# One scan chain, eight buffers for the projected inputs and TensorE-only adaLN slices in a hybrid S5 / DeltaNet / mixture-of-experts layer

## The chip, the cores and the metric

The kernel runs on one core of a Trainium2 chip. A time is the device time of one execution in microseconds (us); several executions are timed and their median is told. One further execution is recorded by the profiler, and all rows below come from that one.

## What is computed

One layer of a trunk, with 512 latent tokens `x` and 256 context tokens `ctx` of width 2048, all in fp32. Cut to what matters here:

```
mod = silu(c) @ ada_w + ada_b            # 2048 x 12288: shift, scale, gate, twice
sh1, sc1, g1, sh2, sc2, g2 = split(mod)
hin  = concat([ctx * (1 + csc1) + csh1, x * (1 + sc1) + sh1])
proj = hin @ w_in                        # first 1024 columns: S5, the rest: DeltaNet
# S5, 64 groups of 16 channels, 64 complex states, forward and backward
bu = einsum(b_bar, u); h[t] = lam_bar * h[t-1] + bu[t]; y = einsum(c_mat, h).real
s5 = g * sigmoid(g @ glu_w + glu_b),  g = gelu(y_forward + y_backward + d_skip * u)
dn = gated_delta_rule(...)               # 8 heads of 128, chunks of 64, both directions
x  = layer_norm(alpha * x + g1 * (concat([s5, dn]) @ w_out))
x  = layer_norm(alpha * x + g2 * expert_choice_ffn(x * (1 + sc2) + sh2))   # 16 experts
```

The context stream itself is not an output; the S5 scans and the DeltaNet recurrences pass through it first.

## The kernel before

The program runs in stages. `phase_in` (0 to some 205 us) makes the first two adaLN vectors (its loads are issued at L281, its matmuls are L284), normalizes the inputs and projects the S5 columns. A projection (helper lines L387 to L398) loads a weight tile `wr`, casts it on ScalarE to `wh` (L388), takes the rest `wl = wr - wh` on GpSimd (L390), and adds three products on TensorE: L396, L397, L398. Beside 512 latent columns (a matmul of 512 columns) some also have 256 context columns.

`put_u` then stores the projected S5 inputs: for each of eight row blocks, ScalarE (L1724) and VectorE (L1725) copy the accumulators into a tile `ue`, and a DMA (L1727) writes it to DRAM. `ue` has two buffers. `transposed` turns B and C coefficients by way of TensorE, a ScalarE copy into `tpd` (two buffers, L909) and a store.

The S5 stage works in blocks of 8 scan positions, 94 of them in a row for context and latent together. `s5_states` (L1108) makes the input of each state: 32 steps of two groups each, with loads of `P` and `B`, products on VectorE (L1124 to L1128) and GpSimd (L1123, L1126), four matmuls L1133 and ScalarE copies into the tile `VH`. `s5_scan` (L1149) goes along `VH`: 94 steps of three VectorE operations, each of which needs the result of the one before (L1156 the product, L1157 and L1158 the two additions). The groups are split into two chains of 32 by the table `CHAINS`: the scan of the first 32 groups follows the first 16 state steps in the program, and the scan of the other 32 the last 16. `s5_local` (L1161, matmuls L1173) and `s5_outputs` (L1177: ScalarE copies `Hs`, 256 matmuls L1192, an addition on VectorE) make the outputs, which go through DRAM (`yd`) to `s5_gelu` (L1219) and `gates` (L490 to L499). In the DeltaNet stage (L572 is the first matmul of its first head, some 805 us) eight heads pass through a front, an inversion and a scan, and the output projection follows. The mixture of experts runs from some 1620 us to the end.

Two kinds of work are filler and are laid beside all this: the DeltaNet projections (a list `PRE` of those that come before the DeltaNet stage, `REST` inside it), and the adaLN slices for `g1, sh2, sc2, g2`: 16 slices of 512 columns (four of the 2048 columns of each). `ada_chunk` loads a slice in eight loads of two row blocks by 512 columns (`aw`, 512 KB each, L213) and multiplies them on TensorE with the vector `cT` in a 128x32 tile of the array (L217); the 16 row blocks go round four column tiles, two at a time. The slices with numbers 2 and 3 (`AV`) go to `ada_vec` instead: 16 multiply-adds of 128x512 on VectorE (L255) and a small matmul.

The order on each engine is not the program's: a scheduler sets it at build time, from the program's dependencies, its pools of buffers and a model of the durations. Any edit in the stages up to 1590 us therefore moves filler about.

Of the kernel before, what the change touches and what calls it, by code (L numbers as in the profile page):

```python
# [11 lines left out]
F32 = mybir.dt.float32  # L12
# [9 lines left out]
D = 2048  # L22
# [19 lines left out]
def ap(t, off, dims):  # L42
    return bass.AP(tensor=t.tensor, offset=t.offset + off, ap=[list(d) for d in dims])
# [6 lines left out]
def mp(K, shape=(128, 4, 128), tag="mp"):  # L50
    return K.ps.tile(list(shape), F32, name=tag, tag=tag, bufs=K.banks[tag])
# [151 lines left out]
    nc.vector.tensor_scalar(K.nega, K.nega, -1.0, None, op0=MUL)  # L203


def ada_chunk(K, I, pool, c0, nk=8, bufs=2):

    nc = K.nc
    src = I["ada_w"]
    pa = mp(K, (128, 512), K.adb)  # L210
    for k0 in range(0, KT, nk):
        aw = pool.tile([128, nk, 512], F32, name="aw", tag="aw", bufs=bufs)
        nc.sync.dma_start(aw, ap(src, c0 + k0 * 128 * 6 * D, [[6 * D, 128], [128 * 6 * D, nk], [1, 512]]))  # L213
        for kk in range(nk):
            k = k0 + kk
            j = k % 4
            nc.tensor.matmul(pa[32 * j:32 * j + 32], K.cT[:, k], aw[:, kk], start=k < 4, stop=k >= 12, tile_position=(0, 32 * j))  # L217
    return pa


def turn(K, pool, pa, pm):
# [9 lines left out]
def ada_cols(K, I, pool, c0, dst, m, **kw):  # L231

    nc = K.nc
    pa = ada_chunk(K, I, pool, c0, **kw)
    pm = mp(K, (128, 512), K.adb)[:, :4 * m].rearrange("p (a b) -> p a b", a=4)
    turn(K, pool, pa, pm)
    cb = c0 // 128
    nc.vector.tensor_tensor(dst, pm, bc(K.cols[:, cb:cb + 4][:, :, None], [128, 4, m]), op=ADD)
    yield from ()


def ada_vec(K, I, pool, c0, dst, m, nk, bufs):

    nc = K.nc
    V = nc.vector
    acc = pool.tile([128, 512], F32, name="part2", bufs=1)
    for k0 in range(0, KT, nk):
        aw = pool.tile([128, nk, 512], F32, name="aw", tag="aw", bufs=bufs)
        nc.sync.dma_start(aw, ap(I["ada_w"], c0 + k0 * 128 * 6 * D, [[6 * D, 128], [128 * 6 * D, nk], [1, 512]]))
        for kk in range(nk):  # L250
            c = K.cT[:, k0 + kk, 0:1]
            if k0 + kk == 0:
                V.tensor_scalar(acc, aw[:, kk], c, None, op0=MUL)
            else:
                V.scalar_tensor_tensor(acc, aw[:, kk], c, acc, op0=MUL, op1=ADD)  # L255
        if AVY:
            yield
    t = pool.tile([128, 512], F32, name="part", bufs=1)
    V.transpose(t, acc)
    r = pool.tile([128, 16, 1], F32, name="part3", bufs=1)  # L260
    V.tensor_reduce(r[:, :, 0], t.rearrange("p (a c) -> p a c", c=32), axis=AX.X, op=ADD)
    pm = mp(K, (128, 4, 1), K.adb)
    for q in range(4):
        nc.tensor.matmul(pm[32 * q:32 * q + 32], K.sel32, r.rearrange("p (a q) m -> p q a m", q=4)[:, q], start=True, stop=True, tile_position=(0, 32 * q))
    cb = c0 // 128
    V.tensor_tensor(dst, pm, K.cols[:, cb:cb + 4][:, :, None], op=ADD)

# [605 lines left out]
BN = 2  # L875
CP = (0, 1)
SV = (999,999,999)
AV = (2, 3)
AVY = 0
MA = (4, (1,))  # L880
YB = 3
STEP0 = [1, 1, 2]
# [1 line left out]
NP = 6  # L884
QZ = [(0, 0), (0, 1)] + [(w, h + (0 if w else 2)) for h in range(6) for w in (3, 0)] + [(3, 6), (3, 7)]
PRE, REST = QZ[:NP], QZ[NP:]
NKA = (2,3)
AR = 2
NWS = 13
PARTS = (0,4),(4,4),(8,4),(12,3),(15,1)  # L890
NN = [0, 2, 2, 0, 0]
UB = 2
NA = sum(NN)
NKB = (2,3)

CHAINS = ((0, 32, "vector"), (32, 32, "vector"))
OPB = 4
AWB = 3
XTB = 1
# [3 lines left out]
def transposed(K, p, src, n, dst):  # L903

    pt = mp(K, (128, n, 128))
    for i in range(n):
        K.nc.tensor.transpose(pt[:, i], src[:, 128 * i:128 * i + 128], K.ident)
    t = p.tile([128, n, 128], F32, name="tpd", bufs=2)
    K.nc.scalar.copy(t, pt)  # L909
    K.nc.sync.dma_start(dst, t)  # L910

# [392 lines left out]
def ada_rest(K, I):  # L1304

    nc = K.nc
    cols = [K.const.tile([128, KT, 1], F32, name=f"ada{s}") for s in range(2, 6)]
    K.g1, K.sh2, K.sc2, K.g2 = cols
    for s, dst in zip(range(2, 6), cols):
        for ch in range(4):  # L1310
            f = ada_vec if 4 * (s - 2) + ch in AV else ada_cols
            yield from f(K, I, K.ada, s * D + ch * 512, dst[:, 4 * ch:4 * ch + 4], 1, nk=K.nka[0], bufs=K.nka[1])
            yield
    nc.vector.tensor_scalar(K.sc2, K.sc2, 1.0, None, op0=ADD)
    yield
# [362 lines left out]
def hybrid_trunk_kernel(tc, I, O):  # L1678
# [3 lines left out]
    with ExitStack() as es:  # L1682
# [36 lines left out]
        K.hin = [(K.yh("hi"), hinl.tile([128, KT, NL], F32R, name="lo")),  # L1719
                 tuple(hinc.tile([128, KT, NC], F32R, name=w) for w in ("hic", "loc"))]  # L1720

        def put_u(i, pl, pc):
            ue = K.up.tile([128, 8, 96], F32, name="ue", bufs=2)
            nc.scalar.copy(ue[:, :, 32:96].rearrange("p s (r w) -> p w s r", r=8), pl.rearrange("p (w s r) -> p w s r", w=8, s=8))  # L1724
            nc.vector.tensor_copy(ue[:, :, 0:32].rearrange("p s k -> p k s"), pc.rearrange("p (k s) -> p k s", s=8))  # L1725
            o = (32 * (i % 2) + i // 2) * 12288
            nc.sync.dma_start(ap(K.us5, o, [[4 * 12288, 8], [768, 16], [1, 768]]), ue.rearrange("p a b -> p (a b)"))  # L1727

        s5k = vk.enter_context(left("s5k"))
        with left("acc") as accp:  # L1730
            uts, par = phase_in(K, I, accp, s5k)
            for i, (pl, pc) in enumerate(uts):
                put_u(i, pl, pc)
        pss.close()
        K.ps = pss.enter_context(tc.tile_pool(name="psx", bufs=1, space=PSUM, reuse_waits="tile"))
        K.adb = "ada"
# [169 lines left out]
```

## Time and profile before

| | us |
|---|---|
| median of three runs (lowest, highest) | 2703.14 (2702.12, 2708.47) |
| the profiled execution | 2703.15 |
| its span in the trace | 2701.4 |
| TensorE busy | 2467.7 (91%) |
| VectorE busy | 1300.9 (48%) |
| ScalarE busy | 717.7 (27%) |
| GpSimd busy | 783.6 (29%) |

The times of the stages in this execution: copies of `put_u` 213.6 to 244.4 us, states 444 to 575, first operation of a scan at 511.4 and last at 687.2, S5 outputs 652.8 to 714.8, first DeltaNet head 805.3, mixture of experts from 1620. A stage's busy times are read from the windows, what an engine waited for from the waits, and the price of one instruction from the timeline. The granted clock of TensorE over the span is 0.96 of its upper level. Ends of matmuls are modelled, so the time from one start to the next tells more than the duration.

### The profile page before, as it was taken

How to read it: one execution, taken by the hardware profiler on the slowest of the kernel's cores; microseconds unless marked ns; L12 is line 12 of the kernel's file. 1: busy time of each engine (PE TensorE's matmuls, PEld its weight loads, DVE VectorE, ACT ScalarE, POOL GpSimd, SP SyncE). 2: the span in 40 equal slices, each digit the busy share in tenths (PEclk: the TensorE clock that was granted, in tenths of full speed). 3: DMA queues.
4: the chain of work that ended last, by engine and by line, in shares of the span. 5: the costliest groups of instructions: out<-in, count | busy, mean ns of one | idle time of the engine just before them, and what ended most of it. 6: DMA issues, size and time to landing. Idle time of an engine off the chain costs nothing. (4 is left out here: it accounts for less than half of the span.)

```text
span 2701.4 us, 41223 instructions
## 1 busy us (share of the span) xinstructions
PE 2467.7 (91%) x16062; PEld 1541.3 (57%) x16062; DVE 1300.9 (48%) x2831; ACT 717.7 (27%) x1611; POOL 783.6 (29%) x747
## 2 busy tenths in 40 slices
PE   7998989899878989899999859999999999999994
PEld 4665778778756766566667724434444444444441
DVE  3362685899577677767877560411111101010106
ACT  2223233534544344443333330201010101010111
POOL 2341275631255464545454410400000000000002
PEclk9998999999988999899999979999999999999997
DMA  9956847766654456777763287998999999999893
GB/s 281 323 176 166 266 148 210 195 163 163 187 158 123 116 174 197 239 224 227 225 194 85 63 319 276 362 382 339 390 384 389 383 390 366 406 366 408 350 406 128
DMA packets 444317, 698.73 MB, mean 259 GB/s; under 512 B 91288, under 2 KB 271001, under 8 KB 443097
## 3 DMA queue, kind: packets, MB, share of 16 engines
q1 hardware_dynamic: 438745, 693.82, 74.6%
q10 hardware_dynamic: 5376, 2.26, 0.4%
q8 instruction: 127, 2.08, 0.3%
q14 instruction: 69, 0.57, 0.1%
HBM read 646.12 MB, written 49.87 MB: 258 GB/s over the span
## 5 line engine op out<-in xcount | busy, mean ns | idle before, releaser
L390 POOL TENSOR_TENSOR wl<-wr,wh 128x512 fp32r<-128x512 f32 (+2 forms) x248 | 335.2, 1354 | 609.3 <-ACT wh L388 577.9
L1522 PE MATMUL mp<-ws,selT 128*64 128x512 f32 x1992 | 468.9, 594 | 0.5 <-ACT selT L1461 0.5
L1522 PEld LDWEIGHTS mp<-ws,selT 128*64 128x64 f32 x1992 | 176.2, 137 | 265.7 <-issue 258.8
L1556 PE MATMUL mp<-ws,hT 128*64 128x512 f32 x896 | 298.2, 603 | 0.0
L1606 POOL TENSOR_TENSOR yp<-ypf,yp 128x512 fp32r<-128x512 f32 x31 | 39.7, 1280 | 875.0 <-ACT yp L1605 875.0
L388 ACT CAST wh<-wr 128x512 fp32r<-128x512 f32 (+2 forms) x249 | 150.5, 605 | 351.3 <-PE pp L397 140.1
L396 PE MATMUL pp<-hi,wh 128*128 128x512 f32 (+1 forms) x528 | 222.0, 420 | 18.4 <-ACT wh L388 18.4
L398 PE MATMUL pp<-hi,wl 128*128 128x512 f32 (+1 forms) x528 | 221.6, 420 | 16.3 <-POOL wl L390 16.3
L397 PE MATMUL pp<-lo,wh 128*128 128x512 f32 (+1 forms) x528 | 217.4, 412 | 0.0
L1528 DVE SCALAR_TENSOR_TENSOR hid<-hid,mp 128x512 f32<-128x512 f32 x16 | 11.0, 688 | 354.9 <-ACT hid L1527 354.1
L1604 DVE SCALAR_TENSOR_TENSOR ypf<-mp,gc,g2r 128x512 f32<-128x512 f32 x32 | 24.0, 751 | 318.5 <-issue 184.9
L1556 PEld LDWEIGHTS mp<-ws,hT 128*64 128x64 f32 x896 | 83.5, 136 | 141.9 <-issue 130.2
L1618 DVE TENSOR_TENSOR acc<-acc,pp 128x512 f32<-128x512 f32 x124 | 79.1, 683 | 162.7 <-PE pp L1616 162.7
L1458 PEld LDWEIGHTS pp<-oh,mixed 128*128 128x128 f32 x1024 | 123.5, 197 | 57.3 <-issue 57.3
L1461 ACT ACTIVATE selT<-pp,colB,colA 128x128 f32<-128x128 f32 x128 | 48.3, 457 | 341.8 <-PE pp L1458 341.8
L1458 PE MATMUL pp<-oh,mixed 128*128 128x128 f32 x1024 | 136.8, 287 | 1.3 <-DVE oh L1450 1.3
L398 PEld LDWEIGHTS pp<-hi,wl 128*128 128x128 f32 (+1 forms) x528 | 102.7, 195 | 49.1 <-POOL wl L390 25.3
L396 PEld LDWEIGHTS pp<-hi,wh 128*128 128x128 f32 (+1 forms) x528 | 104.0, 197 | 37.3 <-ACT wh L388 23.0
L397 PEld LDWEIGHTS pp<-lo,wh 128*128 128x128 f32 (+1 forms) x528 | 104.1, 197 | 18.3 <-issue 4.7
L1527 ACT ACTIVATE hid<-mp 128x512 f32<-128x512 f32 x16 | 9.6, 597 | 381.6 <-PE mp L1522 381.6
L217 PE MATMUL ada<-aw,cT 128*32 128x512 f32 x448 | 100.1, 633 | 11.8 <-DMA aw<-in_ada_w_dram 7.3
L396 PE MATMUL pp<-oph,wh 128*128 128x512 f32 x240 | 98.9, 417 | 6.7 <-DVE Z L666 3.5
(583 smaller groups left out, 4819.2 us busy)
## 6 DMA issues: line engine op xcount, KB each, us to landing
ws<-in_exp_w_dram SPq DMA_DIRECT2D x375, 1024.0 KB
aw<-in_ada_w_dram SPq DMA_DIRECT2D x184, 512.0 KB
wr<-in_w_in_dram SPq DMA_DIRECT2D x157, 256.0 KB
wr<-in_w_out_dram SPq DMA_DIRECT2D x52, 256.0 KB
cl<-CL SPq DMA_DIRECT2D x8, 1024.0 KB
P<-tp SPq DMA_DIRECT2D x32, 256.0 KB
B<-tb SPq DMA_DIRECT2D x32, 256.0 KB
CLo<-cl SPq DMA_DIRECT2D x16, 512.0 KB
```

What stands on the lines that cost most here:

```text
L217: nc.tensor.matmul(pa[32 * j:32 * j + 32], K.cT[:, k], aw[:, kk], start=k < 4, stop=k >= 12, tile_position=(0, 32 * j))
L388: nc.scalar.copy(wh, wr)
L390: (nc.vector if K.nsp % K.sv == 1 else nc.gpsimd).tensor_tensor(wl, wr, wh.bitcast(F32), op=SUB)
L396: T.matmul(out, wh, hi, start=st, stop=False, **kw)
L397: T.matmul(out, wh, lo, start=False, stop=False, **kw)
L398: T.matmul(out, wl, hi, start=False, stop=sp, **kw)
L1458: T.matmul(pg[:, j], K.y[:, k, b], ohf[:, b], start=(b == 0), stop=(b == 3))
L1461: A.activation(S.selT[:, k], pg[:, j], AF.Identity, scale=K.A[:, k:k + 1], bias=K.B[:, k:k + 1])
L1522: T.matmul(acc4[2 * w + c][64 * a:64 * a + 64], S.selT[:, k, 64 * a:64 * a + 64], ws[w, a][:, kk, 512 * c:512 * c + 512], start=(k == 0), ...
L1556: T.matmul(acc[c][64 * a:64 * a + 64], S.hT[:, f0 + f, 64 * a:64 * a + 64], ws[a][:, f, 512 * c:512 * c + 512], start=(f0 + f == 0), stop= ...
L1606: (nc.vector if end else nc.gpsimd).tensor_tensor(t[:, 1], y, t[:, 0].bitcast(F32), op=SUB)
L1618: K.nc.vector.tensor_tensor(K.acc[:, b, s], K.acc[:, b, s], ps, op=ADD)
```

## The change

Four edits. `ada_chunk` goes through each half of 256 columns with four loads of four row blocks by 256 columns (again eight loads of 512 KB for a slice), and the four matmuls of a load use the four column tiles. `ada_vec` goes: all 16 slices take the TensorE way. `CHAINS` holds one chain of 64 groups, so the whole scan stands behind all 32 state steps, and its operations are twice as wide (256, 128 and 128 columns) and half as many. `ue` has eight buffers in a pool of its own that is closed after the stores, and `tpd` four. `ADY` is 0, so the added `yield None` is never reached.

```diff
-def ada_chunk(K, I, pool, c0, nk=8, bufs=2):
+def ada_chunk(K, I, pool, c0, bufs=3):
 
     nc = K.nc
     src = I["ada_w"]
     pa = mp(K, (128, 512), K.adb)
-    for k0 in range(0, KT, nk):
-        aw = pool.tile([128, nk, 512], F32, name="aw", tag="aw", bufs=bufs)
-        nc.sync.dma_start(aw, ap(src, c0 + k0 * 128 * 6 * D, [[6 * D, 128], [128 * 6 * D, nk], [1, 512]]))
-        for kk in range(nk):
-            k = k0 + kk
-            j = k % 4
-            nc.tensor.matmul(pa[32 * j:32 * j + 32], K.cT[:, k], aw[:, kk], start=k < 4, stop=k >= 12, tile_position=(0, 32 * j))
-    return pa
+    for c in range(0, 512, 256):
+        for k0 in range(0, KT, 4):
+            aw = pool.tile([128, 4, 256], F32, name="aw", tag="aw", bufs=bufs)
+            nc.sync.dma_start(aw, ap(src, c0 + c + k0 * 128 * 6 * D, [[6 * D, 128], [128 * 6 * D, 4], [1, 256]]))
+            for j in range(4):
+                nc.tensor.matmul(pa[32 * j:32 * j + 32, c:c + 256], K.cT[:, k0 + j], aw[:, j], start=k0 == 0, stop=k0 == 12, tile_position=(0, 32 * j),
+                                 skip_group_check=True)
+        if ADY:
+            yield None
+    yield pa
...
-    pa = ada_chunk(K, I, pool, c0, **kw)
+    for pa in ada_chunk(K, I, pool, c0, **kw):
+        if pa is None:
+            yield
...
-def ada_vec(K, I, pool, c0, dst, m, nk, bufs):
-
-    nc = K.nc
-    V = nc.vector
-    acc = pool.tile([128, 512], F32, name="part2", bufs=1)
-    for k0 in range(0, KT, nk):
-        aw = pool.tile([128, nk, 512], F32, name="aw", tag="aw", bufs=bufs)
-        nc.sync.dma_start(aw, ap(I["ada_w"], c0 + k0 * 128 * 6 * D, [[6 * D, 128], [128 * 6 * D, nk], [1, 512]]))
-        for kk in range(nk):
-            c = K.cT[:, k0 + kk, 0:1]
-            if k0 + kk == 0:
-                V.tensor_scalar(acc, aw[:, kk], c, None, op0=MUL)
-            else:
-                V.scalar_tensor_tensor(acc, aw[:, kk], c, acc, op0=MUL, op1=ADD)
...
-    V.transpose(t, acc)
...
-AV = (2, 3)
-AVY = 0
+ADY = 0
...
-NKA = (2,3)
+NKA = 3
...
-NKB = (2,3)
-
-CHAINS = ((0, 32, "vector"), (32, 32, "vector"))
+NKB = 3
+
+CHAINS = ((0, 64, "vector"),)
...
-    t = p.tile([128, n, 128], F32, name="tpd", bufs=2)
+    t = p.tile([128, n, 128], F32, name="tpd", bufs=4)
...
-            f = ada_vec if 4 * (s - 2) + ch in AV else ada_cols
-            yield from f(K, I, K.ada, s * D + ch * 512, dst[:, 4 * ch:4 * ch + 4], 1, nk=K.nka[0], bufs=K.nka[1])
+            yield from ada_cols(K, I, K.ada, s * D + ch * 512, dst[:, 4 * ch:4 * ch + 4], 1, bufs=K.nka)
...
-        def put_u(i, pl, pc):
-            ue = K.up.tile([128, 8, 96], F32, name="ue", bufs=2)
+        def put_u(i, pl, pc, pool):
+            ue = pool.tile([128, 8, 96], F32, name="ue", bufs=8)
...
-            for i, (pl, pc) in enumerate(uts):
-                put_u(i, pl, pc)
+            with left("ues") as pool:
+                for i, (pl, pc) in enumerate(uts):
+                    put_u(i, pl, pc, pool)
```

The scheduler then gives another order from about 205 us to about 1590 us. In the rows below the changed kernel has its own line numbers (L1698 is L1724 of before, L364 is L388, L1131 to L1133 are L1156 to L1158, L1099 to L1103 are L1124 to L1128, L216 is L217, L372 to L374 are L396 to L398, L748 is L772).

On ScalarE, the copies into `ue` and the casts of weights among them, before:

```order
L1724 COPY ue<-early 128x8x8x8 x2
L388 CAST wh<-wr 128x512 x2
L1724 COPY ue<-early 128x8x8x8
L388 CAST wh<-wr 128x512
L1724 COPY ue<-early 128x8x8x8
L1724 COPY ue<-accl 128x8x8x8
L388 CAST wh<-wr 128x512
L1724 COPY ue<-accl 128x8x8x8 x2
L388 CAST wh<-wr 128x512
L1724 COPY ue<-accl 128x8x8x8
```

and with the change:

```order
L364 CAST wh<-wr 128x512 x4
L1698 COPY ue<-early 128x8x8x8 x2
L364 CAST wh<-wr 128x512 x2
L1698 COPY ue<-early 128x8x8x8 x2
L364 CAST wh<-wr 128x512
L1698 COPY ue<-accl 128x8x8x8 x2
L364 CAST wh<-wr 128x512
L1698 COPY ue<-accl 128x8x8x8 x2
L364 CAST wh<-wr 128x512
```

The eight copies stand in pairs, closer together, with as many casts among them.

On VectorE, the end of the state steps (operations on `W`) and the scan (operations on `m` and `VH`), before; `VH_3378` is the chain of the first 32 groups:

```order
L1156 TENSOR_TENSOR m_3833<-VH_3378,Lm 128x128
L1157 TENSOR_TENSOR VH_3378<-VH_3378,m_3833 128x64
L1158 TENSOR_TENSOR VH_3378<-VH_3378,m_3833 128x64
L1124 TENSOR_TENSOR W_4432<-P_4428,B_4429 128x256
L1127 TENSOR_TENSOR W_4432<-P_4428,B_4429 128x256
L1156 TENSOR_TENSOR m_3837<-VH_3378,Lm 128x128
L1125 TENSOR_TENSOR W_4432<-W_4432,t_4433 128x256
L1128 TENSOR_TENSOR W_4432<-W_4432,t_4434 128x256
L1157 TENSOR_TENSOR VH_3378<-VH_3378,m_3837 128x64
L1158 TENSOR_TENSOR VH_3378<-VH_3378,m_3837 128x64
L1156 TENSOR_TENSOR m_3841<-VH_3378,Lm 128x128
L1157 TENSOR_TENSOR VH_3378<-VH_3378,m_3841 128x64
```

and with the change, where one `VH_3442` holds all groups:

```order
L1100 TENSOR_TENSOR W_4098<-W_4098,t_4099 128x256
L1103 TENSOR_TENSOR W_4098<-W_4098,t_4100 128x256
L1099 TENSOR_TENSOR W_4119<-P_4115,B_4116 128x256
L1102 TENSOR_TENSOR W_4119<-P_4115,B_4116 128x256
L1100 TENSOR_TENSOR W_4119<-W_4119,t_4120 128x256
L1103 TENSOR_TENSOR W_4119<-W_4119,t_4121 128x256
L1131 TENSOR_TENSOR m_4136<-VH_3442,Lm 128x256
L1132 TENSOR_TENSOR VH_3442<-VH_3442,m_4136 128x128
L1133 TENSOR_TENSOR VH_3442<-VH_3442,m_4136 128x128
L1131 TENSOR_TENSOR m_4140<-VH_3442,Lm 128x256
L1132 TENSOR_TENSOR VH_3442<-VH_3442,m_4140 128x128
L1133 TENSOR_TENSOR VH_3442<-VH_3442,m_4140 128x128
```

Before, steps of the first chain stand among the operations of the last 16 state steps, and the second chain joins later. With the change the last state step is followed by the scan, and nothing but its three operations in a row.

On TensorE, an adaLN slice inside the DeltaNet stage (`pp<-glu` is the S5 gate projection, `scan` a DeltaNet head), before:

```order
L396 MATMUL pp<-glu,wh 128x512
L217 MATMUL ada<-aw,cT 32x512 x2
L397 MATMUL pp<-glu,wh 128x512
L398 MATMUL pp<-glu,wl 128x512
L772 MATMUL scan_9958<-vt,zw_7875 128x128
L217 MATMUL ada<-aw,cT 32x512 x2
L396 MATMUL pp<-glu,wh 128x512
```

and with the change:

```order
L372 MATMUL pp<-glu,wh 128x512
L216 MATMUL ada<-aw,cT 32x256 x4
L748 MATMUL scan_9645<-vt,zw_7562 128x128
L216 MATMUL ada<-aw,cT 32x256 x4
L372 MATMUL pp<-glu,wh 128x512
L373 MATMUL pp<-glu,wh 128x512 x2
L374 MATMUL pp<-glu,wl 128x512
```

A load now brings four matmuls of 256 columns instead of two of 512. Counted over TensorE's order: ahead of the last state step stand 992 projections of 512 columns and 990 of 256 before, 927 and 927 with the change; from there to the first L1192, 162 and 162 before, 347 and 273 with the change; among the L1192, 102 and 48 before, 113 and none with the change; and from the last L1192 to the first DeltaNet head 234 and 139 of 512 columns.

## Rows read from the trace of the kernel before

**Rows 1.** The page, busy us (share of the span) and number of instructions, TensorE
```profile
PE 2467.7 (91%) x16062; PEld 1541.3 (57%) x16062; DVE 1300.9 (48%) x2831; ACT 717.7 (27%) x1611; POOL 783.6 (29%) x747
```

**Rows 2.** Windows (us): their length, then busy us (instructions) of each engine, granted clock, DMA share, GB/s
```profile
444.00:575.00 131.00, 111.73 (x652) 96.48 (x650) 110.67 (x216) 65.57 (x118) 79.08 (x81) 0.93 0.70 193
575.00:687.00 112.00, 107.90 (x677) 96.95 (x676) 105.04 (x484) 37.73 (x53) 22.69 (x17) 0.95 0.71 168
...
715.00:805.00 90.00, 66.37 (x241) 48.36 (x240) 72.98 (x92) 35.83 (x61) 41.96 (x31) 0.88 0.56 154
805.00:1555.00 750.00, 686.11 (x6827) 506.03 (x6828) 538.73 (x1210) 298.86 (x777) 379.17 (x403) 0.95 0.57 170
...
1620.00:2660.00 1040.00, 1024.71 (x4582) 463.70 (x4584) 161.45 (x237) 100.75 (x219) 64.95 (x39) 1.00 0.93 368
```

**Rows 3.** Timeline of TensorE: start us, us, and what ran, three places
```profile
31.26 0.64 PE L284 MATMUL pp<-aw,cT 128*32 128x256 f32 x8 [0.20 <-DMA aw<-in_ada_w_dram]
31.83 0.50 PE L396 MATMUL tr<-hi,wh 128*128 128x512 f32 x1
...
17.52 1.08 PE L284 MATMUL pp<-aw,cT 128*32 128x256 f32 x8 [1.75 <-DMA aw<-in_ada_w_dram]
...
996.63 0.39 PE L398 MATMUL pp<-glu,wl 128*128 128x512 f32 x1
996.86 0.40 PE L396 MATMUL pp<-glu,wh 128*128 128x512 f32 x1
997.18 1.05 PE L217 MATMUL ada<-aw,cT 128*32 128x512 f32 x4
998.17 0.50 PE L397 MATMUL pp<-glu,wh 128*128 128x512 f32 x1
```

**Rows 4.** The page's groups: busy us, mean ns, idle before; adaLN slices on TensorE
```profile
L217 PE MATMUL ada<-aw,cT 128*32 128x512 f32 x448 | 100.1, 633 | 11.8 <-DMA aw<-in_ada_w_dram 7.3
```

**Rows 5.** Line L255: count, duration ns min/median/max, first and last start us
```profile
L255 DVE SCALAR_TENSOR_TENSOR part<-aw,cT,part x30: 750/752/1783, 296.1 to 337.3; 128x512 f32<-128x512 f32 x30
```

**Rows 6.** Waits from 205 to 250 us: us in total, times, longest
```profile
ACT ue L1724 <- DMA us<-ue: 19.6, 6, 7.8
...
PE tr L396 <- DVE accl L375: 6.8, 2, 5.1
```

**Rows 7.** Waits from 444 to 575 us, and line L1133 (as Rows 5)
```profile
DVE W L1124 <- DMA B<-tb: 26.9, 15, 10.2
...
L1133 PE MATMUL mp<-U,W x256: 243/275/530, 447.4 to 574.9; 128*128 128x96 f32 x128
```

**Rows 8.** Timeline of VectorE at the scan's end: start us, us, and what ran
```profile
685.81 0.29 DVE L1156 TENSOR_TENSOR m<-VH,Lm 128x128 f32<-128x128 f32 x1
686.14 0.23 DVE L1157 TENSOR_TENSOR VH<-VH,m 128x64 f32<-128x64 f32 x1
...
686.66 0.29 DVE L1156 TENSOR_TENSOR m<-VH,Lm 128x128 f32<-128x128 f32 x1
```

**Rows 9.** Timeline of VectorE where both chains run side by side
```profile
644.04 1.45 DVE L1157 TENSOR_TENSOR VH<-VH,m 128x64 f32<-128x64 f32 x2
...
645.68 0.48 DVE L1156 TENSOR_TENSOR m<-VH,Lm 128x128 f32<-128x128 f32 x2
646.09 0.34 DVE L1157 TENSOR_TENSOR VH<-VH,m 128x64 f32<-128x64 f32 x2
...
646.63 0.48 DVE L1156 TENSOR_TENSOR m<-VH,Lm 128x128 f32<-128x128 f32 x2
```

**Rows 10.** Timeline of GpSimd at the same place
```profile
643.92 1.35 POOL L390 TENSOR_TENSOR wl<-wr,wh 128x512 fp32r<-128x512 f32 x1 [3.75 <-ACT wh L388]
```

**Rows 11.** Lines L1192 and L572 (as Rows 5), and the L1192 of 640 to 720 us (as Rows 4)
```profile
L1192 PE MATMUL mp<-Hs,CLo 128*128 128x64 f32 x256 | 30.8, 277 | 2.3 <-DMA CLo<-cl 1.2 <-ACT Hs L1189 1.1
...
L1192 PE MATMUL mp<-Hs,CLo x256: 217/275/421, 652.8 to 714.8; 128*128 128x64 f32 x128
...
L572 PE MATMUL front<-ident,kr x48: 270/273/448, 805.3 to 1394.0; 128*128 128x128 f32 x48
```

More of the change, by code (lines that the diff above doesn't have):

```diff
@@ L238, in ada_cols @@
     nc.vector.tensor_tensor(dst, pm, bc(K.cols[:, cb:cb + 4][:, :, None], [128, 4, m]), op=ADD)
-    yield from ()
-def ada_vec(K, I, pool, c0, dst, m, nk, bufs):
-    nc = K.nc
-    V = nc.vector
-    acc = pool.tile([128, 512], F32, name="part2", bufs=1)
-    for k0 in range(0, KT, nk):
-        aw = pool.tile([128, nk, 512], F32, name="aw", tag="aw", bufs=bufs)
-        nc.sync.dma_start(aw, ap(I["ada_w"], c0 + k0 * 128 * 6 * D, [[6 * D, 128], [128 * 6 * D, nk], [1, 512]]))
-        for kk in range(nk):
-            c = K.cT[:, k0 + kk, 0:1]
-            if k0 + kk == 0:
-                V.tensor_scalar(acc, aw[:, kk], c, None, op0=MUL)
-            else:
-                V.scalar_tensor_tensor(acc, aw[:, kk], c, acc, op0=MUL, op1=ADD)
-        if AVY:
-            yield
-    t = pool.tile([128, 512], F32, name="part", bufs=1)
-    V.transpose(t, acc)
[L260 to L266, printed above, removed]
 def ada_pair(K, I, pool, c0, dst, n):
```

## Prediction

> **What bounds the kernel now.** I read the page's busy times first, then the windows by stage, the waits of each stage, and last the timelines for prices. TensorE is busy 91% of the span [rows 1]. The mixture-of-experts part, from 1620 us on, has it at 1024.7 of 1040 us [rows 2]; the change moves nothing there, so all that can move lies ahead. There, TensorE is still busy most of the time (111.7 of 131 us during the S5 states, 107.9 of 112 during the rest of the scans, 686.1 of 750 in the DeltaNet stage, 66.4 of 90 in the gap between), because projections are laid as filler into every chain of short steps [rows 2]. So two quantities count: TensorE's work, and the stretches in which the filler runs out while a chain on another engine goes on. I follow the chain of stages: last state, scan end, last S5 output, first DeltaNet head, end of the DeltaNet stage.
>
> **Prices.** A projection matmul of 512 columns follows the one before it after 0.23 us (996.63 to 996.86) [rows 3]; I take half, 0.116 us, for 256 columns. An adaLN load of two row blocks by 512 columns (4 records, since each fp32 matmul shows as two) holds TensorE from 997.18 to 998.17, 0.99 us; the kernel's first adaLN part already has the changed form, four row blocks by 256 columns (8 records), which holds it from 31.26 to 31.83, 0.57 us [rows 3]. Both read 512 KB. With loads that run back to back, the old form averages 100.1/112 = 0.89 us [rows 4]. For the new one I take 0.60 us; the ends are 0.50 and 1.0 (the second if it costs what the old one does).
>
> **adaLN slices.** Two of 16 slices leave VectorE (L255, 30 operations of about 752 ns, within 296 to 337 us [rows 5]) and go to TensorE. In the S5 stage TensorE then has 32 loads x 0.60 = 19.2 us instead of 16 x 0.89 = 14.3: +5 us. VectorE's 22 us there are not on the chain that ends last: the lag products behind it are bound by several engines, and I give it nothing (up to -8 us if it was late for them). In the DeltaNet stage 12 slices, 96 loads, cost 57.6 instead of 85.8 us: -28 us of TensorE work.
>
> **Projected inputs.** Eight buffers for `ue` and four for `tpd` remove ScalarE's 19.6 us of waiting for the stores (six waits). Of that, TensorE feels only 6.8 us, where its accumulators come free late [rows 6]. But in the changed order the loads of B and C now stand behind all the copies on ScalarE's queue, so I count -6 us, between -9 and +3.
>
> **To the last state.** By the order, 65 projections of 512 and 63 of 256 columns that stood ahead of the last state now stand behind it: -15 - 7, and +5 for the slices: -17 us of TensorE work. The states themselves are bound by their loads (VectorE waits 26.9 us for B [rows 7]), so the absence of scan steps among them gives nothing. The last state, at 574.9 [rows 7], comes at 575 - 17 - 6 = 552.
>
> **One chain.** A chain has 94 steps of three dependent operations. Where one runs alone, a step takes 0.85 us (685.81 to 686.66): 0.33 from the start of the product of 128 columns to the next, and 0.26 for each addition of 64 [rows 8]. So 64 columns more cost 0.066 us; 256 columns take some 0.33 + 0.13 = 0.46 and 128 take 0.33: the wide step is 0.46 + 2 x 0.326 = 1.11 us. Two narrow chains side by side take 0.95 us for a step of both (645.68 to 646.63 [rows 9]), so the wide one isn't cheaper where they ran together: 94 x 1.11 = 104.5 us, against 89. What is lost is the overlap: the first chain ran among the states, and the second beside the outputs. Then there is GpSimd. At 643.92 it starts a split of a weight (L390, 1.35 us [rows 10]), and the scan operations at 644.04 last 1.45 us as a pair instead of 0.34 [rows 9]: 1.1 us lost. Between last state and scan end the kernel before has 17 GpSimd operations [rows 2]; the changed order puts 347 projections of 512 columns, three products times four row blocks to a weight tile, so 12, there: 29 splits, 29 x 1.05 = 30 us. So the scan lasts 135 us (104 if no split delays it). TensorE has 347 x 0.23 + 273 x 0.116 + 16 (128 local outputs at the 31/256 us of L1192 [rows 11]) = 128 us of work in the same stretch, so neither leaves the other much room. Scan end: 552 + 135 = 687, where it is today.
> The Trainium skill ("SBUF — State Buffer", "The single rule") says that VectorE and GpSimd contend for one port pair as an exclusive lock, and that an operation of VectorE with two SBUF inputs takes part in it against a GpSimd operation that reads SBUF. The 0.34 us that became 1.45 agree, and by that rule the scan costs 135 us; without it, 104 us, and TensorE's 128 us would set the stretch.
>
> **Outputs and the gap.** Outputs ran from 652.8 to 714.8 [rows 11], the first half beside the second scan. Now all 256 come after 687, with 113 projections in between: 31 us of busy time [rows 11] + 113 x 0.23 = 57 us, so 745. From the last output to the first DeltaNet matmul it took 805.3 - 714.8 = 90.5 us [rows 11], with VectorE busy for 73.0 of 90 (gelu, then gates) [rows 2]. That chain stays, and its filler shrinks from 234 to 139 projections (54 to 32 us) because the scan ate it; I take 86 us. DeltaNet starts at 745 + 86 = 831, **26 us later** than now (bounds +5 and +40).
>
> **DeltaNet stage.** Its TensorE work falls by 28 us of slices and by the 36 projections that now run earlier (8.4 us): -36.6 us. TensorE is busy for 91% of it, so most of this should shorten the stage; but VectorE is at 72% [rows 2], and where the chain of a head is bare, less filler only leaves a hole. I take two thirds, **-24 us**; bounds 0.2 (-7) and 0.95 (-35).
>
> **Sum.** +26 - 24 = +2 us. The profiled execution took 2703.15 us (2701.4 of span and 1.75 around it), the median of the runs is 2703.14: 2703 + 2 = 2705.
>
> **Rivals.**
> *A: the stage doesn't give it back (slower).* If the heads go by their own chain through TensorE, VectorE and ScalarE, the slices were filler that cost nothing, and cheaper filler buys little. For it: VectorE at 72%, and TensorE idle for 64 us there while filler was at hand. Against it: 91%. At a fifth, -7 us: +19, and with the start a little later (+28) 2724. It decides from the point at which less than half of the 36.6 us comes back (26 - 18 = +8).
> *B: the front ends earlier than I think (faster).* The start of DeltaNet by TensorE's work alone: +5 for slices, +8.4 for projections, less 6 for `ue`: +7, if no new hole opens in the gap and the scan hides under its filler. Then -25 in the stage: -18, 2685. For it: TensorE's work in total falls by 23 us. Against it: 22 us less filler in a gap that VectorE sets.
> *C: the new load isn't cheaper.* The kernel's first such loads, at 9 to 18 us, last 1.08 us [rows 3]. At 1.0 us, 96 loads cost 96 instead of 85.8 us in the stage, which then comes out 2 us longer (10 - 8), and the 32 ahead of it cost 13 us more than I counted: 26 + 13 + 2 = +41, 2744.
>
> **Chances.** Forecast 0.43 (its own range 2693 to 2717), A 0.28, B 0.25, C 0.04. 0.3% (8 us) is about what a measurement of this kernel can tell from no change. Of the forecast's share 0.30 lies within 8 us, 0.04 below, 0.09 above; of A 0.24 is slower and 0.04 within, of B 0.22 faster and 0.03 within; C is slower. Faster 0.26, same 0.37, slower 0.37. Range 2680 to 2732: it leaves out C, the far end of A and the far end of B.
>
> **What would show it.** After: no ScalarE wait at the `ue` copies; last state near 552 and the scan's first step right behind it; scan operations with medians near 411 and 279 ns, some 29 of them stretched by a microsecond; scan end near 687, last output near 745, first head near 831 with a hole in TensorE before it; slices at some 75 to 80 us busy in total; DeltaNet stage near 726 us. Wrong would be: a scan that ends far from 687, a load above 0.8 us, or a stage that keeps its 750 us (A) or loses the whole 37 us.

## The result and the profile after

The changed kernel takes 2725.91 us (median of four runs, 2723.6 to 2727.08) against 2704.14 for the kernel before on the same chip: 1.0077 times as long (95% interval 1.006 to 1.0095), some 22 us slower. The forecast was 2705, no change. The result lies outside the forecast's own range (2693 to 2717) and inside the whole one (2680 to 2732), close to the price of rival A (2724): it is the "slower" to which the prediction gave 0.37.

The table has the ends of the stages in the two profiled executions, and what the prediction gave.

| us | before | forecast | after |
|---|---|---|---|
| last state (last matmul of the states) | 574.9 | 552 | 555.8 |
| scan end (start of its last operation) | 687.2 | 687 | 690.1 |
| last S5 output | 714.8 | 745 | 757.2 |
| first DeltaNet head | 805.3 | 831 | 843.9 |
| first use of the last output projection (L1368, now L1342) | 1554.3 | 1556 | 1578.2 |
| first gather of the experts (L1458, now L1432) | 1619.8 | | 1643.3 |

The page of the kernel after (compare [rows 1]):

```profile
span 2725.0 us, 42055 instructions
PE 2461.2 (90%) x16638; PEld 1558.4 (57%) x16638; DVE 1270.0 (47%) x2515; ACT 717.6 (26%) x1611; POOL 785.1 (29%) x747
```

TensorE is busy 6.5 us less and the span is 23.6 us longer, so it idles 30 us more. Where, the windows of the kernel after say (us, their length, then busy us and instructions of PE (TensorE), PEld (its weight loads), DVE (VectorE), ACT (ScalarE), POOL (GpSimd), granted clock of TensorE, DMA share, GB/s; compare [rows 2]):

```profile
423.00:556.00 133.00, 117.80 (x700) 102.76 (x701) 94.94 (x129) 67.94 (x123) 84.21 (x83) 0.95 0.75 204
557.00:691.00 134.00, 126.46 (x744) 110.59 (x742) 123.37 (x282) 28.26 (x52) 38.05 (x28) 0.99 0.61 136
691.00:757.50 66.50, 63.40 (x370) 57.19 (x371) 7.74 (x18) 41.40 (x44) 13.26 (x11) 0.86 0.58 172
757.50:844.00 86.50, 44.34 (x147) 32.31 (x146) 69.86 (x95) 31.01 (x54) 34.39 (x24) 0.74 0.50 138
844.00:1578.00 734.00, 660.11 (x7174) 506.69 (x7175) 537.19 (x1207) 296.37 (x770) 370.16 (x398) 0.96 0.60 176
...
1643.00:2683.00 1040.00, 1024.33 (x4578) 463.71 (x4580) 161.51 (x238) 100.71 (x219) 64.96 (x39) 0.99 0.93 368
```

The hole is the fourth row: 42 us without work for TensorE between the last output and the first head, where it was 24 in 90 us. The expert part is as long as before. The DeltaNet stage went from 749 to 734 us; its TensorE work fell by 25 (685 to 660), so 10 us of that became idle time.

The scan (lines of the kernel after: count, duration ns min/median/max, first and last start us), with the states and outputs on either side:

```profile
L1108 PE MATMUL mp<-U,W x256: 243/275/530, 435.8 to 555.8; 128*128 128x96 f32 x128
...
L1131 DVE TENSOR_TENSOR m<-VH,Lm x94: 424/426/1535, 557.4 to 689.3; 128x256 f32<-128x256 f32 x94
...
L1132 DVE TENSOR_TENSOR VH<-VH,m x94: 291/293/1407, 557.8 to 689.8; 128x128 f32<-128x128 f32 x94
...
L1167 PE MATMUL mp<-Hs,CLo x256: 221/275/476, 692.6 to 757.2; 128*128 128x64 f32 x128
...
L548 PE MATMUL front<-ident,kr x48: 270/273/448, 843.9 to 1416.2; 128*128 128x128 f32 x48
```

Nothing overlaps any more: the scan starts 1.6 us after the last state, and the outputs 2 us after the scan. Before, the first scan began 63 us ahead of the last state.

A step of the scan, and a GpSimd split within one (timelines of VectorE and of GpSimd after, start us, us; compare [rows 9, 10]):

```profile
600.13 0.42 DVE L1131 TENSOR_TENSOR m<-VH,Lm 128x256 f32<-128x256 f32 x1
600.59 0.29 DVE L1132 TENSOR_TENSOR VH<-VH,m 128x128 f32<-128x128 f32 x1
600.91 0.29 DVE L1133 TENSOR_TENSOR VH<-VH,m 128x128 f32<-128x128 f32 x1
601.24 0.42 DVE L1131 TENSOR_TENSOR m<-VH,Lm 128x256 f32<-128x256 f32 x1
601.70 1.27 DVE L1132 TENSOR_TENSOR VH<-VH,m 128x128 f32<-128x128 f32 x1
...
601.27 1.55 POOL L366 TENSOR_TENSOR wl<-wr,wh 128x512 fp32r<-128x512 f32 x1 [6.96 <-PE pp L374]
```

An undisturbed step takes 601.24 - 600.13 = 1.11 us, as worked out. Of the scan's 282 operations 28 last over 0.8 us, and GpSimd ran 28 splits in the stretch (second window).

### The profile page after: what moved, and what is told of

The parts are those of the page before. It is cut to its first block, busy times and chain, and to the rows that moved or that the text cites. A ratio compares the mean times of both kernels' runs of the same rounds, so it can differ in the third digit from the quotient of the medians.

```text
span 2725.0 us, 42055 instructions
## 1 busy us (share of the span) xinstructions
PE 2461.2 (90%) x16638; PEld 1558.4 (57%) x16638; DVE 1270.0 (47%) x2515; ACT 717.6 (26%) x1611; POOL 785.1 (29%) x747
## 4 chain that ended last, share of the span: by engine, by line
PE 59%; DVE 21%; DMA 10%; issue 3%; POOL 3%; ACT 2%; SPq 2%; DVEq 0%; ACTq 0%; POOLq 0%
PE mp L1496 16%; PE mp L1530 10%; PE pp L1432 5%; PE pp L374 3%; PE pp L372 3%; PE pp L373 3%; DMA B<-tb 3%; PE pp L1590 3%; DMA aw<-in_ada_w_dram 2%; DVE m L1131 2%; PE ada L216 2%; DVE VH L1132 2%; DVE VH L1133 1%; DVE Z L642 1%; DVE tp L641 1%
## 5 line engine op out<-in xcount | busy, mean ns | idle before, releaser
L364 ACT CAST wh<-wr 128x512 fp32r<-128x512 f32 (+2 forms) x249 | 150.1, 605 | 359.3 <-PE pp L373 110.9
L374 PE MATMUL pp<-hi,wl 128*128 128x512 f32 (+1 forms) x528 | 220.4, 418 | 16.0 <-POOL wl L366 15.9
L372 PE MATMUL pp<-hi,wh 128*128 128x512 f32 (+1 forms) x528 | 219.8, 416 | 15.5 <-ACT wh L364 15.4
L1432 PEld LDWEIGHTS pp<-oh,mixed 128*128 128x128 f32 x1024 | 123.5, 197 | 57.3 <-issue 57.3
L1432 PE MATMUL pp<-oh,mixed 128*128 128x128 f32 x1024 | 136.8, 287 | 1.3 <-DVE oh L1424 1.3
L374 PEld LDWEIGHTS pp<-hi,wl 128*128 128x128 f32 (+1 forms) x528 | 103.0, 195 | 46.8 <-POOL wl L366 22.6
L372 PEld LDWEIGHTS pp<-hi,wh 128*128 128x128 f32 (+1 forms) x528 | 103.5, 196 | 34.8 <-ACT wh L364 19.1
L216 PE MATMUL ada<-aw,cT 128*32 128x256 f32 x1024 | 91.4, 404 | 15.7 <-DMA aw<-in_ada_w_dram 15.1
L372 PE MATMUL pp<-oph,wh 128*128 128x512 f32 x240 | 99.1, 417 | 2.6 <-DVE mixed L1269 2.2
```

The lines of the kernel that those rows point to most:

```text
L216: nc.tensor.matmul(pa[32 * j:32 * j + 32, c:c + 256], K.cT[:, k0 + j], aw[:, j], start=k0 == 0, stop=k0 == 12, tile_position=(0, 32 * j), ...
L364: nc.scalar.copy(wh, wr)
L372: T.matmul(out, wh, hi, start=st, stop=False, **kw)
L374: T.matmul(out, wl, hi, start=False, stop=sp, **kw)
L1432: T.matmul(pg[:, j], K.y[:, k, b], ohf[:, b], start=(b == 0), stop=(b == 3))
```

## The experiments

Each run stands beside runs of the kernel before on the same chip; their median was 2707 in these comparisons, so ratios are compared. The theories: (1) the single chain loses the overlap and costs the time; (2) the new adaLN loads cost it; (3) any edit reshuffles the scheduler's order, and single edits don't add up.

| kernel | ratio to before (95%) | last state | last output | first head | DeltaNet stage |
|---|---|---|---|---|---|
| before | 1 | 575 | 715 | 805 | 749 |
| changed | 1.0077 (1.006 to 1.0095) | 556 | 757 | 844 | 734 |
| b_chain | 1.0159 (1.0138 to 1.0181) | 568 | 771 | 855 | 744 |
| b_ada | 1.0028 (1.0011 to 1.0045) | 563 | 700 | 828 | 740 |
| b_ue | 1.0018 (1.0006 to 1.003) | 575 | 717 | 808 | 757 |
| a_chains2 | 1.0014 (0.9999 to 1.0028) | 559 | 697 | 823 | 734 |
| a_ue2 | 1.0111 (1.0094 to 1.0129) | 556 | 754 | 839 | 748 |
| a_hs | 1.0116 (1.0098 to 1.0135) | 557 | 750 | 839 | 748 |
| a_quarter | 1.0021 (1.001 to 1.0032) | 564 | 767 | 846 | 716 |
| b_four | 1.0009 (0.9993 to 1.0024) | 570 | 712 | 826 | 735 |
| b_np4 | 0.9996 (0.9987 to 1.0004) | 573 | 714 | 804 | 750 |
| a_np4 | 1.0071 (1.0053 to 1.009) | 554 | 756 | 836 | 738 |
| a2_np4 | 0.995 (0.9931 to 0.9969) | 560 | 700 | 795 | 751 |
| a2_np2 | 1.0025 (1.0013 to 1.0037) | 567 | 707 | 797 | 773 |

**One chain alone (b_chain), and the changed kernel with two again (a_chains2)**

```diff
 b_chain, from the kernel before      (a_chains2 is the reverse, from the changed kernel)
-CHAINS = ((0, 32, "vector"), (32, 32, "vector"))
+CHAINS = ((0, 64, "vector"),)
```

> The kernel before with one edit: one scan chain of 64 groups. Theory 1 (lost overlap): in the changed kernel 201 us pass from the last state (555.8) to the last S5 output (757.2), before it were 140; the chain alone causes this. With it alone the first DeltaNet head comes some 45 us later than 805, about half of it comes back in the DeltaNet stage, where projections are missing as filler work that ran earlier; total +20 to +30 us. Theory 2 (the new adaLN loads are to blame): +0 to +8 us. Theory 3 (any edit reshuffles the scheduler's order): anything within 10 us.

> The changed kernel with two scan chains of 32 again. Theory 1: the whole loss and more comes back: some 25 to 40 us faster than the changed kernel, so 2686 to 2700, and faster than the kernel before by up to 17. Theory 2: about as slow as the changed kernel, 2715 to 2726. Theory 3: somewhere between 2700 and 2726 that the single edits don't add up to.

The last state and the last output of the two (as above; L1133 and L1192 in b_chain's lines):

```profile
L1133 PE MATMUL mp<-U,W x256: 243/275/529, 448.4 to 567.9; 128*128 128x96 f32 x128
...
L1192 PE MATMUL mp<-Hs,CLo x256: 217/275/476, 708.0 to 771.1; 128*128 128x64 f32 x128
```

```profile
L1108 PE MATMUL mp<-U,W x256: 243/275/499, 433.0 to 559.2; 128*128 128x96 f32 x128
...
L1167 PE MATMUL mp<-Hs,CLo x256: 217/275/476, 636.8 to 697.2; 128*128 128x64 f32 x128
```

b_chain is 1.6% slower (some 43 us), more than any theory gave; going back to two chains takes 0.6% off the changed kernel. So the chain is the loss, and of theory 2 there is at most the 0.28% of b_ada left. The stretch from last state to last output shows where: 203 us in b_chain, 201 in the changed kernel, 198, 193, 202 and 203 in the four other runs with one chain; 138 to 143 in all with two. With one chain, 50 to 65 us are lost there, whatever the other edits are. The cleanest pair is a_np4 and a2_np4 (below), which differ in `CHAINS` alone: 1.0071 and 0.995, 1.2%.

But a_chains2, for which I expected 2686 to 2700, takes 2712.06 and isn't faster than the kernel before, although its outputs end 18 us earlier. Its first head, on VectorE the keys' last operation and on TensorE the first matmul (lines as above):

```profile
L490 DVE SCALAR_TENSOR_TENSOR kr<-raw,kr x8: 929/950/2020, 791.4 to 1320.3; 128x768 f32<-128x768 f32 x8
...
L548 PE MATMUL front<-ident,kr x48: 270/272/475, 822.9 to 1375.6; 128*128 128x128 f32 x48
```

The keys are ready at 792.4 and the head's matmul runs at 822.9. TensorE has projections in between, since its order is fixed when the program is built. In the kernel before keys and head stand at 805.2 and 805.3.

**The adaLN edit alone (b_ada), and the new form of load with two slices still on VectorE (b_four)**

```diff
 b_ada: ada_chunk, ada_cols, NKA, NKB and the call as in the change
 b_four: the same, and
+            if 4 * (s - 2) + ch in AV:
+                yield from ada_vec(..., nk=2, bufs=K.nka)
```

> The kernel before with one edit: all 16 adaLN slices on TensorE, four row blocks by 256 columns a load. Theory 1: faster, -5 to -15 us: TensorE's slices cost 91 instead of 100 us of busy time in all although they are two more, and VectorE loses 22 us of work ahead of the states. Theory 2: slower, +10 to +20 us, because loads with 1 KB rows come late and TensorE waits for them. Theory 3: within 10 us, either sign.

> The kernel before with the new form of load on TensorE (four row blocks by 256 columns), but two slices still on VectorE: TensorE's slices cost some 80 instead of 100 us, and nothing is added ahead of the scans. If less TensorE work in the DeltaNet stage shortens it by 55%, as in the changed kernel: -8 to -12 us against the kernel before. If what made the adaLN edit alone slower was the form of the loads: +5 to +10. If it was the two slices moved to TensorE, the result lies below the kernel before.

b_ada is 0.28% slower where I expected it faster, and b_four the same as before where I expected 8 to 12 us. The loads don't come later in b_ada: TensorE and its weight loads wait 19.0 us for them, 18.7 before. In both kernels the DeltaNet stage shortens (by 9 and 14 us), and in both the first head is late (gap from the last output 128 and 114 us instead of 90) for the reason seen above: its keys are ready at 792.3 and 804.4, and projections stand in front of it until 828 and 826.5. The gain was made and given away by the order.

**The buffers (b_ue, a_ue2)**

```diff
 b_ue: put_u and tpd as in the change
 a_ue2: from the changed kernel, back to two buffers of each
```

> The kernel before with one edit: eight ue buffers in their own pool, four tpd buffers. Theory 1: -3 to -8 us; the copies end some 15 us earlier (229 instead of 244), but TensorE waited only 7 to 9 us for them. Theory 2: the same. Theory 3: within 10 us, either sign.

> The changed kernel with two ue buffers and two tpd buffers again. With one chain the front goes by its chain (keys of the first head ready at 843.7, its matmul at 843.9), so the later copies should count fully, as they can't where TensorE's work sets the front: last state and first head 5 to 12 us later, total +5 to +12 against the changed kernel's 2726. If the buffers are worth nothing in either kernel: within 4 us of it.

The last copy starts at 232 instead of 244 us in b_ue, and the last state stays at 575: nothing came of it, and the kernel is 0.18% slower, with a DeltaNet stage that is 8 us longer. In a_ue2 the last copy starts at 245 again, but last state (556) and head (839) are not the 5 to 12 us later that I expected. Its total is 0.3% longer, as the expectation said, but for another reason: the DeltaNet stage is 14 us longer. So the buffers bring nothing ahead of the DeltaNet stage that these runs show.

**Outputs (a_hs)**

```diff
-        A.copy(Hs[64:128].rearrange(...), VH[64:128, ...])
+        V.tensor_copy(Hs[64:128].rearrange(...), VH[64:128, ...])
```

> The changed kernel with the second of the two copies into Hs on VectorE, which idles after the single scan, instead of on ScalarE. ScalarE's 32 copies of 1.07 us (34 us) with the casts among them set the 65 us of the S5 outputs in the changed kernel: outputs some 8 to 12 us shorter, first head 8 to 12 us earlier, total -5 to -10 us. If TensorE's order sets the outputs: 0.

The outputs shorten by 6.7 us, from 64.6 to 57.9 (692.3 to 750.2), a little less than expected, and the head comes 4 us earlier, half of what I expected. That doesn't show that ScalarE's copies set the outputs: in the changed kernel TensorE is busy for 63.1 of the 64.6 us, and in a_hs the order has 20 projections fewer among the outputs (348 records of TensorE for 368), which at 0.23 us are 4.6 of the 6.7 us. The kernel is slower all the same. The DeltaNet stage after the change, in a_hs and in a_ue2 (three kernels; windows as above, a_hs and a_ue2 from 839 us to their end of the stage and 1 us beyond):

```profile
844.00:1578.00 734.00, 660.11 (x7174) 506.69 (x7175) 537.19 (x1207) 296.37 (x770) 370.16 (x398) 0.96 0.60 176
```

```profile
839.00:1588.00 749.00, 661.83 (x7174) 510.90 (x7175) 526.32 (x1209) 297.13 (x771) 384.34 (x399) 0.94 0.59 169
```

```profile
839.00:1588.00 749.00, 663.06 (x7164) 509.81 (x7164) 525.28 (x1209) 296.30 (x770) 379.96 (x399) 0.93 0.59 169
```

TensorE's work is the same to 3 us, its idle time is 74 us in the first and 86 to 87 in the others. From the first head to the end, the built programs of the changed kernel and of a_hs hold the same matmuls on TensorE, some 7020, with another one in more than half of the places. So it isn't the amount of work that moves this stage by 14 us: theory 3 holds here, and an edit anywhere ahead can cost or give that much. The granted clock is lower in the two slower stages as well (0.94 and 0.93 for 0.96); whether the order makes all of the 14 us by waits or part of it by the clock, these runs don't separate.

**What TensorE's work in the DeltaNet stage is worth (a_quarter)**

```diff
-            for j in range(4):
-                nc.tensor.matmul(..., start=k0 == 0, stop=k0 == 12, ...)
+            for j in range(4 if k0 == 12 else 0):
+                nc.tensor.matmul(..., start=True, stop=True, ...)
```

> The changed kernel with three of four matmul groups of every adaLN slice left out on TensorE (the loads stay; the slices come out wrong). It measures what TensorE's filler work is worth. 68 us of TensorE work go, some 17 of them in the S5 stage and 51 in the DeltaNet stage. If the stages are TensorE's (my forecast counted two thirds), the DeltaNet stage shortens by 34 us or more. If the heads go by their own chain and the slices were filler (rival A), by less than 15 us, and TensorE's idle time there grows by the rest.

Windows of a_quarter's DeltaNet stage, and the slices' part of it (the second row, with its PE and PEld alone); then the slices' part of the changed kernel's:

```profile
846.00:1562.60 716.60, 627.09 (x6597) 504.85 (x6596) 542.75 (x1208) 294.10 (x768) 378.24 (x399) 0.93 0.60 176
...
846.00:1562.60 716.60, 17.62 (x192) 4.24 (x192) 0.93 0.60 176
```

```profile
844.00:1578.00 734.00, 66.61 (x768) 20.10 (x768) 0.96 0.60 176
```

49 us of slice work less (66.6 to 17.6) shorten the stage by 17.4: 0.36 of it. That lies between the two figures expected, nearer to rival A's. But TensorE's idle time grows by 15.6 us alone (73.9 to 89.5), not by all the rest. The other 16 us went into the other matmuls: without the slices, TensorE is busy for 609.5 us with 6405 records (627.1 - 17.6), and in the changed kernel for 593.5 us with 6406 (660.1 - 66.6). The granted clock is 0.93 instead of 0.96. As an estimate, the stage was at the lower of the two clock levels for 2 x (1 - clock) of its length, 100 us instead of 59; a projection takes 0.43 us there instead of 0.23 (rows under the outputs below), so 41 us more at that level lose 19. The clock can so account for all of the 16. Part of the 17 may again be the order.

**The list of projections ahead of DeltaNet (a2_np4, a2_np2, b_np4, a_np4)**

```diff
 a2_np4: from a_chains2      (b_np4 from the kernel before, a_np4 from the changed one; a2_np2 with NP = 2)
-NP = 6
+NP = 4
```

> The changed kernel with two scan chains and four instead of six DeltaNet projections in the list that comes before the DeltaNet stage. In the kernel with two chains, the first head's keys are ready at 792 us but its first matmul runs at 823, behind projections. Theory (TensorE's fixed order delays the head): head at some 804, 19 us of projections move into the holes of the DeltaNet stage, total 5 to 12 us faster than with six, about 2697 to 2703. If the work is the same wherever it runs: within 3 us of the kernel with two chains.

> The kernel before with four instead of six DeltaNet projections in the list ahead of the DeltaNet stage. There the keys of the first head are ready at 805.2 and its matmul runs at 805.3, so nothing is gained by clearing its way: head within 5 us of 805, gap with more idle TensorE, DeltaNet stage 10 to 19 us longer, total 0 to +12 us. If it is the shorter list itself that made the two-chain kernel faster: -5 to -12 us.

> The changed kernel (one chain) with four instead of six projections in that list. Its head goes by the chain, not by projections: head within 5 us of 844, DeltaNet stage 10 to 19 us longer with 19 us more work, unless fewer weight splits in the scan let the scan end earlier (seven fewer: -7 us). Total 0 to +12 us against 2726.

> The changed kernel with two chains and two projections in that list. With four, keys were ready at 795.1 and the head ran at 795.2: the way is clear already, so two fewer only lengthen the DeltaNet stage: head within 5 us of 795, total 0 to +12 us against the 2695.6 of four.

a2_np4 is faster than both kernels: 2695.55 us against 2707.46 for the kernel before, 0.995 times (0.9931 to 0.9969). Keys and head in it, and its gap and stage (lines and windows as above):

```profile
L490 DVE SCALAR_TENSOR_TENSOR kr<-raw,kr x8: 941/948/959, 794.1 to 1298.4; 128x768 f32<-128x768 f32 x8
...
L548 PE MATMUL front<-ident,kr x48: 270/273/447, 795.2 to 1352.6; 128*128 128x128 f32 x48
...
700.00:795.00 95.00, 71.12 (x281) 53.45 (x279) 77.07 (x96) 37.35 (x65) 45.95 (x31) 0.88 0.54 154
795.00:1546.00 751.00, 682.15 (x7280) 525.05 (x7281) 537.70 (x1209) 302.75 (x783) 393.65 (x409) 0.96 0.60 173
```

The head comes 28 us earlier than with six (I expected 19), the stage is 17 us longer, and the total 0.64% lower, more than the 5 to 12 us expected. Against a_chains2, TensorE has 25 us more work in the stage (682 against 657.6) and idles 69 instead of 76 us. b_np4 gives no change and a_np4 next to none (1.0071 against 1.0077), as expected for kernels whose head doesn't stand behind projections. But their stages are 1 and 4 us longer, not 10 to 19, though b_np4 has 11 us more work there (685.4 to 696.0): it went into idle time. a_np4's head is 8 us earlier, not within 5. b_np4 and a2_np4 differ in the adaLN loads and the buffers alone, so with the way of the head clear these two edits gain 0.46% (0.9996 to 0.995), which the runs with six projections hide. a2_np2 leaves the head where it is (797) and lengthens the stage to 773; its 18 us over a2_np4 are more than I expected. TensorE has 17 us more work in that stage (699.1 for 682.2), idles 5 us more, and the way ahead was clear already; whether the order added to it stays open.

## Why the prediction was right, and where it was wrong

The range holds the result because it reached as far as rival A. The forecast itself was 22 us too low, by two sums that erred the same way: the way to the first head and the DeltaNet stage. It got the scan and the gap right.

**Last state** (forecast 552, was 555.8). Right in size, but 6 us of it were given to the wrong cause: the `ue` waits. They are gone (four and four copies, waits for TensorE and VectorE alone):

```profile
L1698 ACT COPY ue<-early x4: 1104/1118/1164, 212.0 to 218.8; 128x512 f32<-128x512 f32 x4
L1698 ACT COPY ue<-accl x4: 1152/1162/1210, 223.0 to 229.3; 128x512 f32<-128x512 f32 x4
its engine sat idle before it (us, times) until:
  PE early L374: 5.6, 2
  DVE accl L351: 2.4, 1
```

b_ue and a_ue2 show no part of the last state's time in it. The other edits moved the states: b_ada alone brings the last state to 563 (570 in b_four, where two slices stay on VectorE), a_chains2 to 559, and b_chain alone to 568. Ahead of the states TensorE now waits 9.2 us for the slices' loads (from 205 to 432 us; 1.8 before, to 450); that the 4 us over the forecast come from these waits is not shown.

**The chain** (135 us forecast, 134 measured). Right in each part: 1.11 us for a step, 28 splits for 29 forecast, some 1.02 us for each ((133 - 94 x 1.11) / 28). The lost overlap as a whole: the forecast had 193 us from last state to last output, the kernels with one chain take 193 to 203.

**The outputs** (57 us forecast, 64.6 measured). This term was mis-sized: I priced TensorE's work at the upper level of its clock. Its filler ran out at 684.9; it idled 7.7 us, until the scan's end and ScalarE's first two copies into `Hs`, and then started the outputs at a granted clock of 0.50, the lower of its two levels (1.2 instead of 2.4 GHz). Windows of the outputs' first part and of the rest, of all outputs, and of those of a_hs; then the timeline of TensorE in the changed kernel:

```profile
692.60:703.00 10.40, 10.37 (x40) 9.64 (x41) 0.84 (x2) 7.08 (x7) 1.28 (x1) 0.50 0.35 110
703.00:757.20 54.20, 52.73 (x329) 47.26 (x328) 6.60 (x16) 32.75 (x35) 11.98 (x10) 0.93 0.64 188
...
692.60:757.20 64.60, 63.10 (x368) 56.89 (x369) 7.44 (x18) 39.83 (x42) 13.26 (x11) 0.86 0.59 175
```

```profile
692.30:750.20 57.90, 56.54 (x348) 51.25 (x348) 18.67 (x32) 21.59 (x25) 11.00 (x9) 0.88 0.66 188
```

```profile
692.63 3.68 PE L1167 MATMUL mp<-Hs,CLo 128*128 128x64 f32 x16 [7.73 <-ACT Hs L1164]
...
701.34 0.63 PE L372 MATMUL pp<-hi,wh 128*128 128x512 f32 x1
701.76 0.63 PE L373 MATMUL pp<-lo,wh 128*128 128x512 f32 x1
...
709.24 0.40 PE L372 MATMUL pp<-hi,wh 128*128 128x512 f32 x1
709.47 0.39 PE L373 MATMUL pp<-lo,wh 128*128 128x512 f32 x1
```

At the lower level a projection follows the one before it after 0.43 us (701.34 to 701.76), at the upper after 0.23. As an estimate, 2 x (1 - 0.86) of the 64.6 us, 18 us, were at the lower level and lost 8.4 of them, so 56 us would have been left: the forecast's 57. The expectation of a_hs, which put the 65 us down to ScalarE's copies, was wrong: TensorE's one wait for them lies ahead of the first output, and from there on it is busy for all but 1.5 us.

**The gap** (86 us forecast, 86.7 measured). Right for one chain (79 to 89 us in the six kernels that have it), where VectorE's chain of gelu, gates and keys sets it: the keys' last operation starts at 842.8 and ends at 843.7, and the head follows at 843.9.

```profile
L490 DVE SCALAR_TENSOR_TENSOR kr<-raw,kr x8: 943/950/1080, 842.8 to 1373.3; 128x768 f32<-128x768 f32 x8
```

That the gap can as well be set by TensorE's order (126 us in a_chains2) I hadn't seen; these runs show it with two chains and the new loads (a_chains2, b_ada, b_four).

**First head** (+26 forecast, +38.6 measured). Of the 13 us, 7 are the outputs, 4 the last state, and 2 the space between scan and outputs, ScalarE's first two copies, for which I had nothing. Rival B (the head 7 us later) is wrong.

**The load** (0.60 us forecast, 66.6 / 96 = 0.69 measured). The form costs what [rows 3] said where it runs whole, but not where the order breaks it up. Timeline of TensorE after:

```profile
1114.88 0.64 PE L216 MATMUL ada<-aw,cT 128*32 128x256 f32 x8
1115.44 0.50 PE L374 MATMUL pp<-glu,wl 128*128 128x512 f32 x1
...
1120.92 0.62 PE L216 MATMUL ada<-aw,cT 128*32 128x256 f32 x2
1121.46 0.50 PE L372 MATMUL pp<-glu,wh 128*128 128x512 f32 x1
```

A whole load holds TensorE for 0.56 us (1114.88 to 1115.44); a single matmul that the order cut off from its load, two records, holds it for 0.54. The slices of the stage went from 84.9 to 66.6 us, 18 us instead of the 28 that I counted. So this term of the stage's sum was mis-sized too. Rival C (a load as dear as before) is wrong.

**The DeltaNet stage** (-24 us forecast, -15 measured). The term that failed most is the work: 36.6 us less were counted, and it fell by only 25 (18 for slices, some 8 for projections). Two thirds of 25 are 17, so that makes 7 of the 9 us. The share makes the other 2: 15 of 25 came back, 0.59; in a_quarter it was 0.36. By the mark in the prediction (less than half of the 36.6 us comes back: 15 are 0.40) rival A decides, but its mechanism, slices that cost nothing, is only part of it. That its 2724 lies beside the 2726 measured is luck: A had the head 28 us later and the stage 7 us shorter, and 39 and 15 were measured. The two errors of the forecast, 13 us at the head and 9 in the stage, have the same sign and make up the 22 us between the forecast and the profiled execution (2725.0 of span and 1.8 around it).

**What stays open.** The three edits don't add up: 1.59, 0.28 and 0.18% alone, 0.77 together. Part of it can be read: with two chains and the new loads (b_ada, b_four, a_chains2) the head stands behind TensorE's projections, so an earlier last state is worth nothing; with one chain the front goes by VectorE's chain, and the 12 us by which the other edits bring the last state forward (568 to 556) reach the head (855 to 844). The other part lies in the DeltaNet stage (744 to 734), and there another order of the same work is worth 14 us, so it can't be given to an edit.

## What to carry to other kernels

A chain of dependent operations that is split in two costs a little more on its engine and lets each half overlap with what feeds it and what follows; joining the halves lost some 60 us of such overlap here to save nothing. The hole that the lost overlap leaves in another engine has a second price: TensorE's granted clock was 0.50 for 10 us behind its 7.7 us hole, so price the work behind a hole at the clock that the rows show there. Where an engine's order is fixed at build time and filled with spare work, look at when the operands of the next chain are ready and when its first instruction runs: 30 us between them hid the gain of the adaLN loads and buffers, and a shorter list of spare work showed it. Filler that is made cheaper pays only a part (0.36 and 0.59 of it here; the rest became idle time and, in a_quarter, slower matmuls), and an edit anywhere can move a scheduled stage by its order (14 us in 734), so measure each edit alone and in company.

## What the runs showed of the hardware

Every weight split on GpSimd that fell into the scan stretched exactly one VectorE operation of two SBUF inputs, from 0.29 or 0.42 to 1.24 to 1.53 us, 28 times of 28; GpSimd had started first each time. That agrees with the exclusive lock in the Trainium skill ("SBUF — State Buffer", "The single rule"); the loss was 1.02 us for a split of some 1.3.

A visit of TensorE to its 128x32 tiles between full-size matmuls costs about the same for one matmul as for four: 0.54 us for two records of 256 columns, 0.56 for eight; the other visits of these two sizes in the stage that ran at the upper clock level held it 0.55 and 0.57. I had not expected that a visit's price goes by its columns and hardly by the number of its matmuls.
